# First stage of a hybrid decoder layer: how h is made, where conditioning is computed, and how its loads are queued

## The chip, the cores and the metric

One core of one Trainium2 chip runs the whole layer. The metric is device time in microseconds of one execution, the median of several runs. TensorE multiplies, VectorE (DVE in the rows), ScalarE (ACT) and GpSimd (POOL) work on rows of up to 128 partitions, and SyncE (SP) issues nearly all transfers.

## The reference

The layer takes x (1024 tokens by 1024 channels) and a conditioning vector c of 1024, all in float32:

```
shift, scale, gate = split(silu(c) @ ada_w + ada_b, 3)
h = rms_norm(x, norm_g) * (1 + scale) + shift
sq, sk, sv, sz, dq, dk, dv, dz, db, da, lq, lk, lv, lz, lr, mg = split(h @ w_in)
out = x + gate * ((g_sb * (y_sb @ proj_sb) + g_gdn * (y_gdn @ proj_gdn) + g_gla * (y_gla @ proj_gla)) @ w_out)
```

`rms_norm(x, g)` is x / sqrt(mean(x^2) + 1e-6) * g. The three mixers y are stick-breaking attention, a gated delta rule and gated linear attention, with four heads each; g_sb, g_gdn, g_gla are sigmoid gates of mg. The change touches only the first two lines, and the part of `h @ w_in` that goes with them.

## The kernel before

**Layout.** Channels lie on partitions and tokens along the row, so x, h and the result are eight tiles (k = 0 to 7) of 128 x 1024. Every large product is done in three passes with operands split in two exact parts: `split` (L149 to L156) lets ScalarE round a tile to `hi` (L151) and VectorE subtract for `lo` (L152).

**The first stage, in order.** SP issues the columns, c and the eight x tiles (L98 to L104). TensorE spreads c over the partitions, ScalarE makes silu of it (`c_row`, L146). The squares of x are made by ScalarE, for two tiles by GpSimd (L315), added in pairs by VectorE (L321), and summed over partitions by products with `ones` (L322): eight float32 products into two banks `ms`. `rstd` is exp(-0.5 ln(.)) on ScalarE (L324, L326).

Then one loop over k. `conditioning(j)` (L295 to L301) loads one 128 x 1024 tile of ada_w, transposed, into a `u6` buffer, of which there are two, and VectorE multiplies it with `c_row` and sums along the row into one column of `mod`; j = k is the shift and j = 8 + k the scale. The weights of the first delta-rule head for this k (four groups of 128 columns) come into one of three `raw` buffers (L339) and are split. The h tile is x times `rstd` on GpSimd (L363), then scaled and shifted on VectorE (L364) and split; tile 0 is done in halves without GpSimd (L353 to L358). TensorE then does 24 products of 512 columns per k: four groups, two halves, three passes, into eight banks. All h tiles stay in the 16 buffers of the tag `h` until the last projection.

**Behind the stage.** The eight banks are copied out, VectorE makes a causal convolution (L383, L386), and a small projection gives the gates of the delta rule (`small_evac`, L451 to L453 with GpSimd; Sigmoid, Exp and Ln on ScalarE; a scan, L473), whose transposes (`gates`, L122) and the tasks of the mixers follow, with the dense projections of the later heads as filler.

**What sets the order.** TensorE's instructions stand in the order in which the program writes them; for the mixers that order comes from estimated costs added up in `clock`, counted from the end of the first stage. The other engines and SP get an order from a planner that simulates the program and issues what it finds ready, in the program's order where several are; each engine then works through its list strictly in order. A buffer of a tag is given to the next tile of that tag once all users of an older one are done.

Of the kernel before, what the change touches and what calls it, by code (L numbers as in the profile page):

```python
# [12 lines left out]
F32 = mybir.dt.float32  # L13
# [6 lines left out]
P = 128  # L20
D = 1024
# [18 lines left out]
for _name, _n in (("norm_g", 8), ("ada_b", 24), ("sb_qnorm", 1), ("sb_knorm", 1), ("conv", 48),  # L40
                  ("gdn_onorm", 1), ("gla_b", 4), ("gla_onorm", 2), ("merge_b", 24),
                  ("a_log", 1), ("dt_bias", 1)):
    COLS[_name] = sum(v[1] for v in COLS.values()), _n
# [9 lines left out]
def kernel(ctx: ExitStack, tc: tile.TileContext, xT: bass.AP, c: bass.AP,  # L53
                             adaT: bass.AP, w_in: bass.AP, cols: bass.AP, consts: bass.AP,
# [44 lines left out]
    crow = big("u3")  # L99
# [39 lines left out]
    na = cp.tile([P, 1], F32, name="na")  # L139
    nc.scalar.activation(out=na[DA, :], in_=C("a_log")[DA, :], func=AF.Exp)  # L140
# [84 lines left out]
    # a dense group: (load, run); loads are issued one group ahead  # L225
# [77 lines left out]
    warm = cp.tile([P, 1], F32, name="warm")  # L303
    nc.scalar.activation(out=warm, in_=c_row[:, 0:1], func=AF.Square)
    nc.scalar.activation(out=warm, in_=warm, func=AF.Ln, bias=one_c)
    rstd = big("u5")
    ms = [bank(pl, "lv", HALF) for _ in range(2)]
    for k in range(KT):
        if k % 2 == 0:
            x2s = big("u4" if k < 4 else "u5")  # L310
        for hf in range(2):
            sl = slice(hf * HALF, (hf + 1) * HALF)
            if k % 2 == 0:
                if k in (2, 4):
                    nc.gpsimd.tensor_mul(out=x2s[:, sl], in0=xs[k][:, sl], in1=xs[k][:, sl])  # L315
                else:
                    nc.scalar.activation(out=x2s[:, sl], in_=xs[k][:, sl], func=AF.Square)
                continue
            x2 = mid(f"v{k // 2 % 2}")
            nc.scalar.activation(out=x2, in_=xs[k][:, sl], func=AF.Square)  # L320
            nc.vector.tensor_add(out=x2s[:, sl], in0=x2s[:, sl], in1=x2)  # L321
            mm(ms[hf], ones, x2s[:, sl], 858, start=(k == 1), stop=(k == KT - 1))  # L322
    for hf in range(2):
        nc.scalar.activation(out=rstd[:, hf * HALF:(hf + 1) * HALF], in_=ms[hf], func=AF.Ln,  # L324
                             scale=1.0 / D, bias=eps_c)
    nc.scalar.activation(out=rstd, in_=rstd, func=AF.Exp, scale=-0.5)  # L326
    amp = cp.tile([P, KT], F32, name="amp")

    # the first head's four column groups advance together as h arrives
# [3 lines left out]
               (pl, "lv"), (pl, "lv"))  # L333
    for k in range(KT):
        conditioning(k)
        conditioning(8 + k)
        raw = raw_tile()
        wsrc = w_in[k * P:(k + 1) * P, O_DQ:O_DQ + 4 * 512].rearrange("p (g n) -> p g n", g=4)
        nc.sync.dma_start(out=raw, in_=wsrc[:, :, 0:P])  # L339
        w = wp.tile([P, 2, 4, P], F32R, tag="w", name="w")  # L340
        if k == 0:
            nc.gpsimd.tensor_copy(out=w[:, 0], in_=raw)
            nc.vector.tensor_sub(out=w[:, 1], in0=raw, in1=w[:, 0].bitcast(F32))
        else:
            split(w[:, 0], w[:, 1], raw)
# [4 lines left out]
        if k == 0:  # L350
            for hf in range(2):
                sl = slice(hf * HALF, (hf + 1) * HALF)
                nc.vector.scalar_tensor_tensor(out=xs[k][:, sl], in0=xs[k][:, sl],  # L353
                                               scalar=amp[:, k:k + 1], in1=rstd[:, sl],
# [105 lines left out]
    for _ in run_cm(small_w, small_evac):  # L460
        pass
# [922 lines left out]
```

## Time and profile before

| | us |
|---|---|
| three runs | 1521.94, 1521.08, 1520.1 |
| median | 1521.08 |
| the profiled execution, first to last instruction | 1522.0 |
| TensorE busy in it | 1463.0 |
| VectorE, ScalarE, GpSimd busy | 861.8, 676.8, 175.8 |

The profiled execution has a span only, no time of its own beside it; the span lies 0.9 us above the median of the runs. Matmul rows overlap, so busy time of TensorE says that it has work, not how fast it works; the distance between the starts of two rows says that. A float32 product has two rows, one of the three-pass products one. "Idle before <-releaser" is the wait of an engine ahead of a row and what ended it.

### The profile page before, as it was taken

How to read it: one execution, taken by the hardware profiler on the slowest of the kernel's cores; microseconds unless marked ns; L12 is line 12 of the kernel's file. 1: busy time of each engine (PE TensorE's matmuls, PEld its weight loads, DVE VectorE, ACT ScalarE, POOL GpSimd, SP SyncE). 2: the span in 40 equal slices, each digit the busy share in tenths (PEclk: the TensorE clock that was granted, in tenths of full speed). 3: DMA queues.
4: the chain of work that ended last, by engine and by line, in shares of the span. 5: the costliest groups of instructions: out<-in, count | busy, mean ns of one | idle time of the engine just before them, and what ended most of it. 6: DMA issues, size and time to landing. Idle time of an engine off the chain costs nothing.

```text
span 1522.0 us, 26560 instructions
## 1 busy us (share of the span) xinstructions
PE 1463.0 (96%) x10564; PEld 1227.5 (81%) x10564; DVE 861.8 (57%) x1855; ACT 676.8 (44%) x1473; POOL 175.8 (12%) x306
## 2 busy tenths in 40 slices
PE   4898999999999999999999999999999999999998
PEld 1677787777778887978888999889988888888887
DVE  5978736557653666667666525563555226474621
ACT  4255845462652846556475524342444442322200
POOL 4231222223330000000000100000000000000000
PEclk8899999999999999999999999999999999999999
DMA  6644322131231211212121212111122334353342
GB/s 211 189 119 120 99 87 74 44 88 47 79 93 50 56 43 53 53 32 60 50 67 38 69 49 63 49 36 42 43 69 85 110 104 138 115 149 111 120 143 76
DMA packets 162470, 126.48 MB, mean 83 GB/s; under 512 B 23429, under 2 KB 139269, under 8 KB 162346
## 3 DMA queue, kind: packets, MB, share of 16 engines
q1 hardware_dynamic: 162202, 124.47, 27.9%
q8 instruction: 83, 1.36, 0.4%
q14 instruction: 41, 0.34, 0.1%
q10 hardware_dynamic: 144, 0.31, 0.1%
HBM read 99.80 MB, written 24.95 MB: 82 GB/s over the span
## 4 chain that ended last, share of the span: by engine, by line
PE 81%; DVE 9%; ACT 4%; POOL 2%; issue 2%; DMA 2%; SPq 0%; POOLq 0%; DVEq 0%; ACTq 0%
PE acc L95 66%; PE lv L95 6%; PE mx L95 6%; PE tr L122 3%; DVE u L299 1%; DVE w L152 1%; POOL c L284 1%; DVE u L386 1%; POOL u L453 1%; DVE w L570 1%; DVE w L572 1%; DVE u L1110 1%; DMA u<-in_adaT 1%; POOL w L596 0%; DMA w<-xd 0%
## 5 line engine op out<-in xcount | busy, mean ns | idle before, releaser
L95 PE MATMUL acc<-h_hi,w 128*128 128x512 f32 x1856 | 658.1, 409 | 12.4 <-ACT h_hi L151 5.7
L95 PEld LDWEIGHTS acc<-h_hi,w 128*128 128x128 f32 x1856 | 352.5, 190 | 84.5 <-ACT h_hi L151 6.1
L95 PE MATMUL acc<-h_lo,w 128*128 128x512 f32 x928 | 365.9, 394 | 8.1 <-DVE h_lo L358 7.7
L95 PEld LDWEIGHTS acc<-h_lo,w 128*128 128x128 f32 x928 | 176.9, 191 | 36.9 <-DVE h_lo L358 8.9
L95 PE MATMUL acc<-whi,h_hi 128*128 128x256 f32 x640 | 186.8, 292 | 0.0
L95 PE MATMUL acc<-whi,h_lo 128*128 128x256 f32 x640 | 180.7, 282 | 0.0
L95 PE MATMUL acc<-wlo,h_hi 128*128 128x256 f32 x640 | 180.7, 282 | 0.0
L95 PE MATMUL acc<-u,w 128*128 128x512 f32 x768 | 176.5, 391 | 0.0
L95 PEld LDWEIGHTS acc<-u,w 128*128 128x128 f32 x768 | 144.2, 188 | 31.6
L151 ACT CAST w<-raw 128x512 fp32r<-128x512 f32 x143 | 84.2, 619 | 121.8 <-PE acc L95 90.4
L152 DVE TENSOR_TENSOR w<-raw,w 128x512 fp32r<-128x512 f32 x143 | 98.5, 701 | 50.7 <-ACT w L151 49.9
L95 PEld LDWEIGHTS acc<-whi,h_hi 128*128 128x128 f32 x640 | 122.3, 191 | 1.4 <-issue 0.7
L95 PEld LDWEIGHTS acc<-wlo,h_hi 128*128 128x128 f32 x640 | 122.4, 191 | 0.1
L95 PEld LDWEIGHTS acc<-whi,h_lo 128*128 128x128 f32 x640 | 122.1, 191 | 0.0
L284 POOL TENSOR_TENSOR c<-c,mhalf 128x4 f32<-128x4 f32 (+1 forms) x56 | 54.7, 976 | 578.8 <-DVE c L282 577.4
L95 PE MATMUL acc<-m_hi,w 128*128 128x512 f32 x256 | 79.0, 389 | 0.0
L1110 DVE TENSOR_TENSOR_SCAN u<-u,zero_c 128x128 f32<-128x128 f32 (+7 forms) x32 | 43.4, 1356 | 36.1 <-ACT u L1108 36.1
L155 DVE SCALAR_TENSOR_TENSOR w<-raw,col,w 128x128 fp32r<-128x128 f32 x96 | 29.5, 349 | 55.3 <-ACT w L154 55.3
L95 PEld LDWEIGHTS mx<-r,u 128*128 128x128 f32 x288 | 44.1, 190 | 18.0 <-DVE r L751 4.9
L95 PEld LDWEIGHTS acc<-m_hi,w 128*128 128x128 f32 x256 | 48.0, 188 | 10.0
L95 PE MATMUL mx<-r,u 128*128 128x128 f32 x288 | 48.5, 281 | 6.3 <-POOL u L720 2.7
L95 PE MATMUL lv<-u,u 128*32 128x32 f32 (+5 forms) x528 | 49.2, 252 | 4.1 <-DVE u L653 4.1
(254 smaller groups left out, 2177.6 us busy)
## 6 DMA issues: line engine op xcount, KB each, us to landing
raw<-in_w_in SPq DMA_DIRECT2D x160, 256.0 KB, 3.0
u<-in_adaT SPq DMA_DIRECT2D x24, 512.0 KB, 3.5
g_dram<-v SPq DMA_DIRECT2D x36, 256.0 KB, 2.1
v<-g_dram SPq DMA_DIRECT2D x36, 256.0 KB, 2.6
u<-in_xT SPq DMA_DIRECT2D x16, 512.0 KB, 5.6
u<-y_dram SPq DMA_DIRECT2D x16, 512.0 KB, 3.8
v<-gam_d SPq DMA_DIRECT2D x16, 256.0 KB, 3.5
y_dram<-v SPq DMA_DIRECT2D x16, 256.0 KB, 2.0
```

Of the source, the lines that this page charges most:

```text
L95: return nc.tensor.matmul(out, lhsT=lhsT, rhs=rhs, **kw)
L122: nc.tensor.transpose(out=out, in_=in_, identity=ident[:k, :k])
L151: nc.scalar.copy(out=hi, in_=raw)
L152: nc.vector.tensor_sub(out=lo, in0=raw, in1=hi.bitcast(F32))
L155: nc.vector.scalar_tensor_tensor(out=lo, in0=raw, scalar=scale, in1=hi.bitcast(F32), op0=ALU.mult, op1=ALU.subtract)
L284: nc.gpsimd.tensor_tensor(out=out, in0=out, in1=mhalf[:, 0:n], op=ALU.pow)
L299: nc.vector.tensor_tensor_reduce(out=junk, in0=aw, in1=c_row, scale=1.0, scalar=0.0, op0=ALU.mult, op1=ALU.add, accum_out=mod[:, j:j + 1])
L386: nc.vector.scalar_tensor_tensor(out=t, in0=r[:, tap:tap + T], scalar=C("conv", j + tap), in1=t, op0=ALU.mult, op1=ALU.add)
L453: nc.gpsimd.tensor_scalar(out=gt[0][DA, sl], in0=raw[DA, :], scalar1=C("dt_bias")[DA, :], scalar2=None, op0=ALU.add)
L570: nc.vector.tensor_tensor(out=t3, in0=L3[:, w:16, j:w].broadcast_to([32, n, w]), in1=Xl3[:, j:w, 0:w].broadcast_to([32, n, w]), op=ALU.mult)
L572: nc.vector.tensor_sub(out=Xl3[:, w:16, 0:w], in0=Xl3[:, w:16, 0:w], in1=t3)
L1110: nc.vector.tensor_tensor_scan(om[:, 0:n][:, ::-1], om[:, 0:n][:, ::-1], zero_c.broadcast_to([P, n]), 1.0, ALU.mult, ALU.add)
```

## The change

- c is loaded as eight columns too (`c_col`), with silu on ScalarE; `crow` moves to a `u8` buffer. `na` (Exp) is computed later, ahead of the gates' Sigmoid.
- The squares: tile 0 on GpSimd, tiles 1 and 3 on VectorE, the others on ScalarE. Tiles 0, 1 and 2 go to TensorE alone, 3 to 5 as one sum, 6 and 7 as one sum in halves: ten products. `rstd` is Sqrt on ScalarE and `reciprocal` on VectorE, by halves; a one-column Sqrt (`root`) stands after the first squares.
- The conditioning tiles are loaded into buffers of the tag `h`, two per k, the first three pairs with their raw weights ahead of the loop. For k = 0 and 1 the tile comes in another layout (`adaP`) and TensorE multiplies it with `c_col`: eight products of one moving column per tile, into the one bank of the tag `tr`, ahead of the first h products. For k = 2 to 7 VectorE reduces as before, in place, with one addition for shift and scale.
- h is made for every k as it was for tile 0: VectorE multiplies x by amplitude and `rstd` in one instruction, ScalarE adds the shift and rounds, VectorE makes the low part from x, shift and `hi`. GpSimd has no part in it, nor in the split of tile 0's weights.

```diff
@@ columns: c also comes as eight columns of 128
-                  ("a_log", 1), ("dt_bias", 1)):
+                  ("a_log", 1), ("dt_bias", 1), ("c", 8)):
...
-    crow = big("u3")
+    crow = big("u8")
...
-    na = cp.tile([P, 1], F32, name="na")
-    nc.scalar.activation(out=na[DA, :], in_=C("a_log")[DA, :], func=AF.Exp)
+    c_col = cp.tile([P, KT], F32, name="c_col")
+    nc.scalar.activation(out=c_col, in_=C("c", 0, KT), func=AF.Silu)
...
-    warm = cp.tile([P, 1], F32, name="warm")
-    nc.scalar.activation(out=warm, in_=c_row[:, 0:1], func=AF.Square)
-    nc.scalar.activation(out=warm, in_=warm, func=AF.Ln, bias=one_c)
+    ms = [bank(pl, "lv", HALF) for _ in range(2)]
+    halves = [slice(hf * HALF, (hf + 1) * HALF) for hf in range(2)]
+    root = cp.tile([P, 1], F32, name="root")
+    def square(k, out, eng):
+        for sl in halves if k == KT - 1 else (slice(0, T),):
+            if eng is nc.scalar:
+                eng.activation(out=out[:, sl], in_=xs[k][:, sl], func=AF.Square)
+            else:
+                eng.tensor_mul(out=out[:, sl], in0=xs[k][:, sl], in1=xs[k][:, sl])
+        return out
+    def add_up(x2, start=False, stop=False):
+        for hf, sl in enumerate(halves):
+            mm(ms[hf], ones, x2[:, sl], 858, start=start, stop=stop)
+    for k, eng in ((0, nc.gpsimd), (1, nc.vector), (2, nc.scalar)):
+        add_up(square(k, big(("u4", "u4", "u5")[k]), eng), start=(k == 0))
+    nc.scalar.activation(out=root, in_=one_c, func=AF.Sqrt)
+    part, more = square(3, big("u6"), nc.vector), [big("u6"), big("u5")]
+    for k in (4, 5):
+        nc.vector.tensor_add(out=part, in0=part, in1=square(k, more[k - 4], nc.scalar))
+    add_up(part)
+    last = [square(k, big("u3"), nc.scalar) for k in (6, 7)]
     rstd = big("u5")
-    ms = [bank(pl, "lv", HALF) for _ in range(2)]
-    for k in range(KT):
-        if k % 2 == 0:
-            x2s = big("u4" if k < 4 else "u5")
-        for hf in range(2):
-            sl = slice(hf * HALF, (hf + 1) * HALF)
-            if k % 2 == 0:
-                if k in (2, 4):
-                    nc.gpsimd.tensor_mul(out=x2s[:, sl], in0=xs[k][:, sl], in1=xs[k][:, sl])
-                else:
-                    nc.scalar.activation(out=x2s[:, sl], in_=xs[k][:, sl], func=AF.Square)
-                continue
-            x2 = mid(f"v{k // 2 % 2}")
-            nc.scalar.activation(out=x2, in_=xs[k][:, sl], func=AF.Square)
-            nc.vector.tensor_add(out=x2s[:, sl], in0=x2s[:, sl], in1=x2)
-            mm(ms[hf], ones, x2s[:, sl], 858, start=(k == 1), stop=(k == KT - 1))
-    for hf in range(2):
-        nc.scalar.activation(out=rstd[:, hf * HALF:(hf + 1) * HALF], in_=ms[hf], func=AF.Ln,
-                             scale=1.0 / D, bias=eps_c)
-    nc.scalar.activation(out=rstd, in_=rstd, func=AF.Exp, scale=-0.5)
+    for hf, sl in enumerate(halves):
+        nc.vector.tensor_add(out=last[0][:, sl], in0=last[0][:, sl], in1=last[1][:, sl])
+        mm(ms[hf], ones, last[0][:, sl], 858, start=False, stop=True)
+        nc.scalar.activation(out=rstd[:, sl], in_=ms[hf], func=AF.Sqrt, scale=1.0 / D, bias=eps_c)
+        nc.vector.reciprocal(out=rstd[:, sl], in_=rstd[:, sl])
+    na = cp.tile([P, 1], F32, name="na")
     amp = cp.tile([P, KT], F32, name="amp")
 
-    # the first head's four column groups advance together as h arrives
+    PRE = 2
+    first_mod = bank(pt, "tr", HALF)
+    def both(ap, k):
+        return ap[:, k:k + 9:8]
+    def conditioning2(k):
+        tiles = [hp.tile([P, T], F32, tag="h", name="ada") for _ in range(2)]
+        if k < PRE:
+            for i, t in enumerate(tiles):
+                nc.sync.dma_start(out=t, in_=adaP[2 * k + i])
+            return lambda: by_product(k, tiles)
+        for i, t in enumerate(tiles):
+            j = 8 * i + k
+            nc.sync.dma_start(out=t, in_=adaT[j * P:(j + 1) * P, :])
+        return lambda: by_rows(k, tiles)
+    def by_product(k, tiles):
+        for i, t in enumerate(tiles):
+            at = 2 * k + i
+            for kk in range(KT):
+                mm(first_mod[:, at:at + 1], t[:, kk * P:(kk + 1) * P], c_col[:, kk:kk + 1], 120,
+                   start=(kk == 0), stop=(kk == KT - 1))
+        nc.vector.tensor_add(out=both(mod, k), in0=first_mod[:, 2 * k:2 * k + 2],
+                             in1=both(C("ada_b", 0, 24), k))
+    def by_rows(k, tiles):
+        for i, t in enumerate(tiles):
+            j = 8 * i + k
+            nc.vector.tensor_tensor_reduce(out=t, in0=t, in1=c_row, scale=1.0, scalar=0.0,
+                                           op0=ALU.mult, op1=ALU.add, accum_out=mod[:, j:j + 1])
+        nc.vector.tensor_add(out=both(mod, k), in0=both(mod, k), in1=both(C("ada_b", 0, 24), k))
     first = (O_DQ, O_DK, O_DV, O_DZ)
     f_ps = [[None, None] for _ in first]
     f_banks = ((pa, "acc"), (pa, "acc"), (pm, "mx"), (pm, "mx"), (pt, "tr"), (pl, "lv"),
                (pl, "lv"), (pl, "lv"))
+    raws, conds = [], []
     for k in range(KT):
-        conditioning(k)
-        conditioning(8 + k)
+        conds.append(conditioning2(k))
         raw = raw_tile()
         wsrc = w_in[k * P:(k + 1) * P, O_DQ:O_DQ + 4 * 512].rearrange("p (g n) -> p g n", g=4)
         nc.sync.dma_start(out=raw, in_=wsrc[:, :, 0:P])
+        raws.append(raw)
+        if k == 2:
+            break
+    for k in range(PRE):
+        conds[k]()
+    for k in range(KT):
+        if k >= 3:
+            conds.append(conditioning2(k))
+            raw = raw_tile()
+            wsrc = w_in[k * P:(k + 1) * P, O_DQ:O_DQ + 4 * 512].rearrange("p (g n) -> p g n", g=4)
+            nc.sync.dma_start(out=raw, in_=wsrc[:, :, 0:P])
+            raws.append(raw)
+        if k >= PRE:
+            conds[k]()
         w = wp.tile([P, 2, 4, P], F32R, tag="w", name="w")
-        if k == 0:
-            nc.gpsimd.tensor_copy(out=w[:, 0], in_=raw)
-            nc.vector.tensor_sub(out=w[:, 1], in0=raw, in1=w[:, 0].bitcast(F32))
-        else:
-            split(w[:, 0], w[:, 1], raw)
+        split(w[:, 0], w[:, 1], raws[k])
         nc.vector.scalar_tensor_tensor(out=amp[:, k:k + 1], in0=mod[:, 8 + k:9 + k], scalar=1.0,
                                        in1=C("norm_g", k), op0=ALU.add, op1=ALU.mult)
         hi = hp.tile([P, T], F32R, tag="h", name="h_hi")
         lo = hp.tile([P, T], F32R, tag="h", name="h_lo")
-        if k == 0:
-            for hf in range(2):
-                sl = slice(hf * HALF, (hf + 1) * HALF)
-                nc.vector.scalar_tensor_tensor(out=xs[k][:, sl], in0=xs[k][:, sl],
-                                               scalar=amp[:, k:k + 1], in1=rstd[:, sl],
-                                               op0=ALU.mult, op1=ALU.mult)
-                nc.scalar.activation(out=hi[:, sl], in_=xs[k][:, sl], func=AF.Identity,
-                                     bias=mod[:, k:k + 1])
-                nc.vector.scalar_tensor_tensor(out=lo[:, sl], in0=xs[k][:, sl],
-                                               scalar=mod[:, k:k + 1],
-                                               in1=hi[:, sl].bitcast(F32),
-                                               op0=ALU.add, op1=ALU.subtract)
-        else:
-            nc.gpsimd.tensor_mul(out=xs[k], in0=xs[k], in1=rstd)
-            nc.vector.tensor_scalar(out=xs[k], in0=xs[k], scalar1=amp[:, k:k + 1],
-                                    scalar2=mod[:, k:k + 1], op0=ALU.mult, op1=ALU.add)
-            split(hi, lo, xs[k])
+        for sl in halves if k == 0 else (slice(0, T),):
+            nc.vector.scalar_tensor_tensor(out=xs[k][:, sl], in0=xs[k][:, sl],
+                                           scalar=amp[:, k:k + 1], in1=rstd[:, sl],
+                                           op0=ALU.mult, op1=ALU.mult)
+            nc.scalar.activation(out=hi[:, sl], in_=xs[k][:, sl], func=AF.Identity,
+                                 bias=mod[:, k:k + 1])
+            nc.vector.scalar_tensor_tensor(out=lo[:, sl], in0=xs[k][:, sl],
+                                           scalar=mod[:, k:k + 1],
+                                           in1=hi[:, sl].bitcast(F32),
+                                           op0=ALU.add, op1=ALU.subtract)
...
+    nc.scalar.activation(out=na[DA, :], in_=C("a_log")[DA, :], func=AF.Exp)
     nc.scalar.activation(out=rows[DB, :], in_=rows[DB, :], func=AF.Sigmoid)
...
+    ada = a["ada_w"][0].reshape(KT, P, 24, P).transpose(2, 1, 0, 3).reshape(24, P, D)
...
+             "adaP": ada[[0, 8, 1, 9]]
```

## Rows read from the trace of the kernel before

**Rows 1.** The profiled page: busy time by engine, and TensorE in 40 slices (tenths)
```profile
PE 1463.0 (96%) x10564; PEld 1227.5 (81%) x10564; DVE 861.8 (57%) x1855; ACT 676.8 (44%) x1473; POOL 175.8 (12%) x306
...
PE   4898999999999999999999999999999999999998
```

**Rows 2.** Stretches: us, busy (x count) of PE, PEld, DVE, ACT, POOL; clock, DMA share, GB/s
```profile
20.00:40.00 20.00, 7.42 (x16) 3.98 (x15) 17.01 (x12) 6.71 (x9) 14.97 (x7) 0.68 0.29 83
...
400.00:1522.00 1122.00, 1108.64 (x8132) 949.24 (x8130) 591.94 (x1216) 475.53 (x1044) 59.21 (x117) 1.00 0.25 75
```

**Rows 3.** The chain of waits, 0 to 135 us: start, us, what
```profile
31.83 5.51 DVE h_lo L358 x2
37.34 3.30 DVE u L299
```

**Rows 4.** VectorE in order of time: start, us, line, operation [idle before <-releaser]
```profile
18.73 1.21 DVE L299 CUSTOM_DVE_ANT_0 u<-u,u 128x1024 f32<-128x1024 f32 x1
...
59.98 0.81 DVE L364 TENSOR_SCALAR u<-u,amp,mod 128x1024 f32<-128x1024 f32 x1
60.71 1.22 DVE L299 CUSTOM_DVE_ANT_0 u<-u,u 128x1024 f32<-128x1024 f32 x1
61.91 1.23 DVE L152 TENSOR_TENSOR h_lo<-u,h_hi 128x1024 fp32r<-128x1024 f32 x1
```

**Rows 5.** GpSimd in order of time
```profile
10.06 2.04 POOL L315 TENSOR_TENSOR u<-u 128x512 f32<-128x512 f32 x2 [8.03 <-DMA u<-in_xT]
...
25.61 20.58 POOL L363 TENSOR_TENSOR u<-u,u 128x1024 f32<-128x1024 f32 x7 [5.03 <-ACT u L326]
```

**Rows 6.** TensorE's products and weight loads (PEld) in order of time
```profile
15.25 7.19 PE L95 MATMUL lv<-u,ones 128*128 128x512 f32 x14 [0.48 <-DVE u L321]
17.11 0.20 PEld L95 LDWEIGHTS lv<-u,ones 128*128 128x128 f32 x1 [0.52 <-issue]
...
21.41 0.19 PEld L95 LDWEIGHTS lv<-u,ones 128*128 128x128 f32 x1 [0.24 <-issue]
...
27.33 0.74 PE L95 MATMUL acc<-h_hi,w 128*128 128x512 f32 x1 [4.89 <-ACT h_hi L356]
...
49.59 0.80 PE L95 MATMUL acc<-h_hi,w 128*128 128x512 f32 x1 [5.69 <-ACT h_hi L151]
...
58.02 0.39 PE L95 MATMUL acc<-h_hi,w 128*128 128x512 f32 x1
...
90.66 0.39 PE L95 MATMUL acc<-h_hi,w 128*128 128x512 f32 x1
```

**Rows 7.** ScalarE in order of time
```profile
7.47 1.15 ACT L317 ACTIVATE u<-u 128x512 f32<-128x512 f32 x2 [3.56 <-DMA u<-in_xT]
...
22.47 0.69 ACT L324 ACTIVATE u<-lv,eps_c 128x512 f32<-128x512 f32 x1 [0.17 <-PE lv L95]
23.18 1.28 ACT L326 ACT_TABLE_LOAD   x1
24.47 1.06 ACT L326 ACTIVATE u<-u 128x1024 f32<-128x1024 f32 x1
```

**Rows 8.** TensorE, products of 128 moving columns, later
```profile
142.11 1.05 PE L95 MATMUL lv<-u 128*128 128x128 f32 x8
```

**Rows 9.** Stretches of 4 us, columns as in rows 2
```profile
8.00:12.00 4.00, 0.00 (x0) 0.00 (x0) 0.34 (x1) 3.95 (x8) 1.94 (x2) 1.00 1.02 417
...
36.00:40.00 4.00, 2.88 (x7) 2.12 (x7) 4.00 (x2) 0.00 (x0) 4.00 (x3) 0.50 0.00 0
```

**Rows 10.** VectorE's groups by line and shape: busy, mean ns, idle before
```profile
L386 DVE SCALAR_TENSOR_TENSOR u<-u,col,u 128x1024 f32<-128x1024 f32 x36 | 46.1, 1291 | 0.1
```

**Rows 11.** The gates' chain behind the stage, GpSimd and TensorE
```profile
100.84 8.96 POOL L453 TENSOR_SCALAR u<-v,col 4x512 f32<-4x512 f32 x1
...
132.40 1.09 PE L122 MATMUL tr<-cst,u 128*128 128x128 f32 x4 [4.68 <-DVE gam_c L490]
```

**Rows 12.** DMA issues, 0 to 60 us: count, KB each, median us to landing
```profile
u<-in_adaT SPq DMA_DIRECT2D x10, 512.0 KB, 3.5
```

More of the change, by code (lines that the diff above doesn't have):

```diff
@@ L53 @@
 def kernel(ctx: ExitStack, tc: tile.TileContext, xT: bass.AP, c: bass.AP,
-                             adaT: bass.AP, w_in: bass.AP, cols: bass.AP, consts: bass.AP,
+                             adaP: bass.AP, adaT: bass.AP, w_in: bass.AP, cols: bass.AP, consts: bass.AP,
                              gla_w2: bass.AP, proj_sb: bass.AP, proj_gdn: bass.AP,
@@ L1361, in _columns @@
              "gla_onorm": tiles(a["gla_onorm"][0]), "merge_b": tiles(a["merge_b"][0]),
-             "a_log": rows(a["gdn_a_log"][0]), "dt_bias": rows(a["gdn_dt_bias"][0])}
+             "a_log": rows(a["gdn_a_log"][0]), "dt_bias": rows(a["gdn_dt_bias"][0]), "c": tiles(a["c"][0])}
     return np.concatenate([parts[n] for n in COLS], axis=1)
@@ L1367 @@
     a = {n: np.asarray(v) for n, v in inputs.items()}
-    feeds = {"xT": a["x"][0].T, "c": a["c"], "adaT": a["ada_w"][0].T, "w_in": a["w_in"][0],
+    ada = a["ada_w"][0].reshape(KT, P, 24, P).transpose(2, 1, 0, 3).reshape(24, P, D)
+    feeds = {"xT": a["x"][0].T, "c": a["c"], "adaP": ada[[0, 8, 1, 9]], "adaT": a["ada_w"][0].T, "w_in": a["w_in"][0],
              "cols": _columns(a), "consts": _constants(), "gla_w2": a["gla_w2"][0],
```

## The prediction

> **What bounds the kernel now.** I read the page first, the stretches second, the chain of waits third, and last the single rows of each engine. The page has TensorE busy for 96% of the span, and its lowest digits stand in the first slices [rows 1]. By stretches [rows 2], TensorE is busy for 7.4 of 20 us between 20 and 40 us and for 1108.6 of the last 1122. So the kernel is bound by TensorE nearly everywhere, and the first 58 us are where it waits. A microsecond won there reaches the end if nothing behind it gives it back, for TensorE's instructions stand in a fixed order.
>
> The chain of waits in that gap [rows 3] is VectorE's: two L358 take 5.51 us, one L299 takes 3.30, before the h of the second tile. The reader is to see that these are slow copies of cheap instructions. L299 takes 1.22 at 60.71; L358 makes half a row in 2.76 us, while at 61.91 a whole row of h_lo takes 1.23 [rows 4]. GpSimd explains it: seven L363 products run from 25.61 to 46.19, 2.94 us each [rows 5], and VectorE's instructions are stretched for as long. TensorE starts the first tile at 27.33, the second at 49.59 and the third at 58.02; from there a tile follows every 5.44 us (32.64 for six, 58.02 to 90.66, where the eighth ends) [rows 6].
>
> **The sum, part by part.**
>
> *The sum of squares.* The x tiles land about 1.3 us apart: GpSimd's squares wait for the third tile until 10.06 [rows 5], and the first square starts at 7.47 [rows 7]. By that spacing the eighth lands at 7.47 + 7 x 1.295 = 16.5. Now there are eight products with `ones`, two rows each, and the last 14 rows end at 22.44 [rows 6]; ten weight loads take 4.30 us from 17.11 to 21.41, so a product takes 0.86. After the change there are ten, but six of them (k = 0, 1, 2) can run while x still arrives, two take the sum of tiles 3 to 5, and only two wait for tiles 6 and 7. GpSimd's one square is now a whole row, two of the 1.02 us halves in rows 5, and the first product waits for it until about 9.6; six products, the first two at half rate, 1.7 us, end near 16.5; the pair of the middle sum near 18.2. For the last pair the path is half a square 0.57 (1.15 for two [rows 7]), half an addition 0.7 (a whole-row two-tensor instruction is 1.23 [rows 4]), and the product, which queues behind the middle pair: 18.2 + 0.86 = 19.1 and 19.9 for the halves.
>
> *The root.* Ln, a table load and Exp take 22.47 to 25.53 now [rows 7]. Afterwards: Sqrt per half, 0.69 as Ln has now, and a reciprocal on VectorE. The trace has no reciprocal. Its bounds are half of L364's whole-row 0.81 us, so 0.4, and the slowest 512-wide row, L358's 2.76 [rows 3, 4]; I take 0.75, near the 0.7 of half an addition, the plainest row of that width. The table for Sqrt is asked for early by `root`; at worst its 1.28 us [rows 7] stand in ScalarE's gap between the last square (17.7) and 19.1. Inverse roots: 20.5 and 21.4.
> The Trainium skill (ScalarE: Activation LUTs, What ACT_TABLE_LOAD costs) puts a switch of tables at about 1283 ns and a further drain of about 1380 ns. Here Exp starts at 24.47, 0.01 us after the load that began at 23.18, so the trace shows the first part and no drain behind it. By the page the removed load would be worth 1.4 us more; I go by the row.
>
> *Conditioning of tiles 0 and 1 on TensorE.* It takes four L299 reductions (1.2 us each where undisturbed) from VectorE and adds 32 one-column products to TensorE, ahead of the first tile's. No such product is in the trace. The nearest are four products of 128 moving columns, two rows each, in 1.05 us [rows 8], 0.26 per product; that is the upper bound at full rate, twice it at half rate, and zero the lower. I take 0.12, about half the upper, because the stationary operand has the same width and the moving one is nearly gone: 2 us for a tile's 16. The first tile's loads have landed by 18.73, when L299 reads them [rows 4]. The second's come after 0.25 + 1.0 MB more; at the 417 GB/s of rows 9 and the slower rate of the 512-byte pieces behind it, near 22.1. So tile 0's products run 19.9 to 21.9 and tile 1's 22.1 to 24.1. Everything on TensorE behind them waits, first of all the first tile.
>
> *The first tile.* After 21.9: addition and amplitude 0.15 and 0.16, two hand-overs 0.2, half a row of x times rstd 0.7 and h_hi 0.7 (half of 1.23 and Ln's 0.69 [rows 4, 7]): 23.8. TensorE's own order gives 24.1. Loads, the split of the weights on ScalarE instead of GpSimd, and the order in VectorE's queue can each put some tenths between; I take 25.0 (24 to 29).
>
> *The tiles after it.* Two tiles cost 10.9 us plus a slow start. Between 36 and 40 us, after long idling, the granted clock is 0.50 (the 1.2 GHz level), and the second tile, begun at 49.59 after 5.7 us without work, took 8.43 instead of 5.44 [rows 6, 9], some of it waiting for h_lo. I add 2.5 once. The second tile ends at 25.0 + 10.9 + 2.5 = 38.4, where it ends at 58.0 now: 19.6 won.
>
> *Can the rest keep the 5.44 pace?* VectorE per tile k = 2 to 7, each a little under its row's length because neighbours overlap: two reductions 2.3, additions and amplitude 0.3, weights' low part 0.6, L364's 0.7 replaced by a two-tensor instruction of a whole row (L386's kind, 1.29 long [rows 10], 1.2 in a sequence), h_lo 1.15: 5.6, against 5.44. That loses 1 us over six tiles, and tiles 0 and 1, without reductions, take about 3.3 each and put it some 4 ahead, which covers it. GpSimd is then out of the way; without that cover, the loss would be the 1 us. Loads: 1.25 MB per tile at 417 GB/s is 3.2 us, under 5.44. The price of queueing ahead is that raw weights from k = 3 on stand behind them in SP's queue: the last conditioning load would land near 38, and VectorE wants the fourth tile's weights near 37, about 8 before TensorE does; this costs VectorE 1 to 2 us of its head start and TensorE nothing.
>
> *Behind the stage.* TensorE meets the gates' chain next: GpSimd's L453 takes 8.96 us, and the transposes at 132.40 wait 4.68 [rows 11]. These hang on the end of the first stage and move with it. Moved `na` adds one Exp (0.2) and perhaps a table load 1.28 to ScalarE around it, and other instructions find a new order. I book 1.5 lost; from 0 (it lies in ScalarE's idle time) to 4.7 (as much again as the wait now).
>
> Sum: 58.0 - 38.4 - 1.5 = 18.1 won. The profiled span is 1522.0 us, 0.9 above the median 1521.1 and the highest listed run is 1521.9; no time around the span is shown, so I subtract from the median: **1503.0**. Its own range, 24 to 27 for the first tile and 0 to 4 behind: 1500 to 1508.
>
> **Rivals.**
>
> *The reciprocal is slow.* If half a row takes 2.8 us, like L358 now, instead of 0.75, two stand in VectorE's queue ahead of the first tile: 19.8 + 5.6 = 25.4, then 0.3 + 0.7 + 0.7, and the first tile starts at 27.3 or a little later, 2.5 to 3 later than above: 1506. For: nothing in the trace shows a division to be as cheap as a product. Against: the simple VectorE rows of this width take 0.7.
> The Trainium skill (VectorE: DVE Perf Modes, First, the fixed hardware budget) speaks for it: reciprocal is an iterative division with a repeat count of 8. An estimate from that page, eight cycles for each of 512 elements at 0.96 GHz, is 4.3 us a half; no run here shows it yet, and the first tile would start near 30, 5 us late, 1508.
>
> *The gain is given back behind the stage.* ScalarE's and VectorE's queues around the gates' chain come out worse by as much as L453's 8.96 us: half the gain goes, 1512. For: that chain waits on GpSimd, ScalarE and VectorE in turn and nothing there is spare. Against: it starts from TensorE's results, and its instructions are the same.
>
> *The loads do not run ahead (the other side).* If a conditioning load waits until the tile before it has given up its h buffer, each of six tiles is a loop: landing 3.5 [rows 12], two reductions 2.4, 0.3 for addition and amplitude, x times rstd 1.29, h_hi 1.1 (two half rows on ScalarE), h_lo 1.2: 9.8. From tile 1's h at 30.8 that ends at 89.6, plus 5.44 for TensorE: 95.1 against 90.66, so 1526, slower. It decides from 9.1 us per tile. For: 32 tiles of that tag pass through 16 buffers. Against: sixteen buffers hold all sixteen conditioning tiles, and two come free for each tile's pair.
>
> *It changes nothing*: the stage is bound by loads anyway. Against: the 4 MB of x have landed at 16.5, and rows 9 have no traffic at all between 36 and 40.
>
> **How the numbers follow.** Forecast 0.60, slow reciprocal 0.20, given back 0.11, loads not ahead 0.05, nothing 0.04. About 0.2% (3 us) is what a measurement of this kernel can tell from no change. The first three are faster and all but a few hundredths of "given back" stay so: 0.90 faster; 0.04 the same; 0.06 slower. The range takes in the start at 24 with a fast clock, 4 us below the forecast with a little gained behind the stage (1498), and reaches up to the given-back case (1512).
>
> **What would show it.** No L363-like products on GpSimd and no VectorE instruction of a whole row above 1.3 us after 20 us; the last `ones` product ends near 20; the first tile starts near 25 and the third near 38; 5.44 us per tile after that; the eighth ends near 72. A reciprocal far over 0.75, an h chain that waits for `in_adaT`, or a third tile later than 44 would prove steps wrong; so would a stage that ends at 72 with an end above 1508.

## The result and the profile after

The changed kernel is slower: 1534.4 us (median of 4 runs, 1534.0 to 1535.5) against 1520.6 for the kernel before on the same chip, ratio 1.0089 with an interval of 1.0074 to 1.0103. Forecast were 1503.0. The profiled execution took 1534.0 us, of which 1532.2 are the span.

The page hides the loss: TensorE is busy for 97% of the span, more than before [rows 1]. By stretches of 20 us (columns as in [rows 2]) TensorE of the kernel before was busy for 7.42 and 13.85 of 20 us in the first two of these and full from 60 to 100 us; after the change none of the four is full.

```profile
20.00:40.00 20.00, 16.86 (x72) 14.40 (x72) 16.77 (x22) 4.75 (x8) 0.20 (x2) 0.57 0.47 153
40.00:60.00 20.00, 16.75 (x66) 13.15 (x66) 14.75 (x26) 3.97 (x5) 0.00 (x0) 0.93 0.62 206
60.00:80.00 20.00, 12.96 (x42) 9.23 (x40) 14.64 (x28) 3.44 (x4) 0.00 (x0) 0.82 0.50 170
80.00:100.00 20.00, 14.66 (x47) 10.94 (x47) 13.24 (x25) 3.80 (x7) 2.33 (x2) 0.83 0.49 149
```

GpSimd's column (the fifth) is nearly empty: its 15 us of products are gone, as the change says. TensorE's rows, in order of time, answer to [rows 6]:

```profile
16.54 2.74 PE L95 MATMUL lv<-u,ones 128*128 128x512 f32 x6
19.12 3.63 PE L95 MATMUL tr<-c_col,ada 128*128 128x1 f32 x32
23.00 6.99 PE L95 MATMUL tr<-c_col,ada 128*128 128x1 f32 x32 [0.25 <-DVE mod L361]
32.27 0.79 PE L95 MATMUL acc<-h_hi,w 128*128 128x512 f32 x1 [2.28 <-ACT h_hi L406]
42.17 0.39 PE L95 MATMUL acc<-h_hi,w 128*128 128x512 f32 x1
47.61 0.39 PE L95 MATMUL acc<-h_hi,w 128*128 128x512 f32 x1
55.02 0.51 PE L95 MATMUL acc<-h_hi,w 128*128 128x512 f32 x1 [1.80 <-ACT h_hi L406]
68.29 0.80 PE L95 MATMUL acc<-h_hi,w 128*128 128x512 f32 x1 [4.25 <-ACT h_hi L406]
79.06 0.50 PE L95 MATMUL acc<-h_hi,w 128*128 128x512 f32 x1 [1.80 <-ACT h_hi L406]
89.54 0.50 PE L95 MATMUL acc<-h_hi,w 128*128 128x512 f32 x1 [1.41 <-ACT h_hi L406]
100.32 0.51 PE L95 MATMUL acc<-h_hi,w 128*128 128x512 f32 x1 [2.32 <-ACT h_hi L406]
108.48 0.39 PE L95 MATMUL acc<-h_hi,w 128*128 128x512 f32 x1
```

The `ones` products end at 19.28 (forecast 19.9). The h tiles k = 0 to 7 start at 32.27, 42.17, 47.61, 55.02, 68.29, 79.06, 89.54 and 100.32, and the eighth ends at 108.48. The third starts 10.4 us earlier than before (58.02), and then the pace of 5.44 is lost: 60.9 us for six tiles instead of 32.6 (a tile's time runs here from its first product to the first of the next). By the fifth tile the lead is gone: 68.29, before 58.02 + 2 x 5.44 = 68.90. The stage ends 17.8 us later than at 90.66.

Against the forecast the span is 28.3 us late (1532.2 for 1522.0 - 18.1 = 1503.9). The third tile was expected at 38.4 and starts at 47.61: 9.2 late, 7.3 of them with the first tile (25.0, measured 32.27). The six tiles after it cost 28.2 more than 32.6. Behind the stage 9.1 came back: from its end to the end of the span are 1423.7 us, before 1431.3, and I had booked 1.5 the other way. 9.2 + 28.2 - 9.1 = 28.3.

The head, in VectorE's row, then the granted clock (last column but two) in two stretches of it and in one of a later tile:

```profile
23.06 6.56 DVE L333 RECIPROCAL u<-u 128x512 f32<-128x512 f32 x2
```
```profile
20.00:24.00 4.00, 3.75 (x30) 3.66 (x29) 1.18 (x3) 1.13 (x3) 0.00 (x0) 0.87 1.05 376
24.00:28.00 4.00, 4.00 (x21) 4.00 (x20) 4.00 (x2) 0.62 (x1) 0.00 (x0) 0.50 0.63 210
...
68.00:72.00 4.00, 3.15 (x7) 2.16 (x8) 1.80 (x5) 0.24 (x1) 0.00 (x0) 0.50 0.63 229
```

A half of the reciprocal is 3.28 us. The one-column products of tile 0 take 3.63, those of tile 1 take 6.99 at half the clock, and both chains end near 30.

Of the 28.2 us lost over the six tiles, TensorE waits 11.6 ahead of tiles 3 to 7 (the five waits for h_hi above) and 5.2 behind their first products for h_lo. Most of the other 11.4 it is busy, but slower: behind such a wait the granted clock is 0.50 for a part of the tile, and over tiles 3 to 7 its mean is 0.67 to 0.81. A slow tile also ends later, and the couplings below hang on the end of a tile.

For the later tiles the chain of waits from 63 us on shows what a tile hangs on:

```profile
64.13 0.63 ACT w L151
64.78 0.69 DVE w L152
...
65.77 1.29 DVE u L403
67.06 1.14 DVE u L299
...
77.34 0.63 ACT w L151
77.99 0.70 DVE w L152
78.71 0.38 SPq L163
...
79.14 0.50 SPq L352
...
79.69 5.64 DMA ada<-in_adaT
85.36 1.23 DVE ada L367
```

Three couplings stand in it. **B**: the split of the weights of tile 6 (L151 on ScalarE, L152 on VectorE) needs a weight buffer that TensorE gives back with the end of tile 3, and it stands ahead of x times rstd (L403) of tile 4 on VectorE; the reductions of tile 4 were done at 62.6. **A**: the conditioning pair of tile 6 (L352 at 79.14) stands on SP behind raw weights (L163), whose buffer L152 frees; so it too hangs on the end of a tile, and then comes 5.64 us of landing and the whole h. **C**: reductions for the output gates (L299), work of the next stage, stand in VectorE's queue between L403 and h_lo, and their loads (L297) on SP ahead of pairs. In that place on VectorE they cost next to nothing (h_hi of tile 6 ends at 89.5, and h_lo starts at 89.56); what costs is their loads on SP. SP's rows show how late the first of the later pairs goes out (the forecast had the last one landing near 38): the raw weights of tiles 3 to 6 are all ahead of the pair of tile 3, though the program asks for that pair first. SP's own waits from 10 to 112 us (us in all, times, longest) show why: 31.9 us for raw weights' buffers, 3.6 for a pair's own buffer, and besides 13.1 in two rows of the gates' loads (L297):

```profile
43.80 0.39 SPq L392 DMA_DIRECT2D raw<-in_w_in  x1
44.23 0.97 SPq L352 DMA_DIRECT2D ada<-in_adaT  x2
```
```profile
SPq L392 <- DVE w L152: 19.7, 4, 10.3
SPq L163 <- DVE w L152: 12.2, 2, 6.9
...
SPq L352 <- DVE mod L367: 3.6, 1, 3.6
```

### The profile page after: what moved, and what is told of

It is laid out like the page before. It is cut to its first block, busy times and chain, and to the rows that moved or that the text cites. A ratio compares the mean times of both kernels' runs of the same rounds, so it can differ in the third digit from the quotient of the medians.

```text
span 1532.2 us, 26643 instructions
## 1 busy us (share of the span) xinstructions
PE 1480.8 (97%) x10632; PEld 1241.6 (81%) x10632; DVE 851.6 (56%) x1839; ACT 676.5 (44%) x1468; POOL 148.6 (10%) x295
## 4 chain that ended last, share of the span: by engine, by line
PE 80%; DVE 9%; ACT 3%; issue 3%; DMA 3%; POOL 2%; SPq 0%; POOLq 0%; DVEq 0%; ACTq 0%
PE acc L95 64%; PE lv L95 6%; PE mx L95 6%; PE tr L122 2%; DVE u L431 2%; PE tr L95 1%; DVE w L152 1%; DVE w L616 1%; DVE w L618 1%; POOL c L284 1%; DMA v<-gam_d 1%; DMA raw<-in_w_in 1%; DVE u L1156 0%; DMA xd<-w 0%; POOL w L642 0%
## 5 line engine op out<-in xcount | busy, mean ns | idle before, releaser
L151 ACT CAST w<-raw 128x512 fp32r<-128x512 f32 x144 | 84.9, 619 | 149.8 <-PE acc L95 90.3
L152 DVE TENSOR_TENSOR w<-raw,w 128x512 fp32r<-128x512 f32 x144 | 97.5, 688 | 56.5 <-ACT w L151 55.8
```

What stands on the lines that cost most here:

```text
L151: nc.scalar.copy(out=hi, in_=raw)
L152: nc.vector.tensor_sub(out=lo, in0=raw, in1=hi.bitcast(F32))
```

## The experiments

All but the last change the changed kernel; ratios are to the kernel before, run on the same chip. Gains against the changed kernel (ratio 1.0089, another chip) go by the ratios. An edit of place or order also lets the planner order the other instructions anew, so none of them moves one thing only.

**One coupling at a time.** First the pairs of all eight tiles are asked for ahead of the first h tile:

```diff
     for k in range(KT):
         conds.append(conditioning2(k))
+        if k >= 3:
+            continue
         raw = raw_tile()
...
-        if k == 2:
-            break
...
         if k >= 3:
-            conds.append(conditioning2(k))
             raw = raw_tile()
```


> All sixteen conditioning tiles are allocated and their loads issued before the first h tile, instead of three pairs ahead and the others each behind the h of the tile before; nothing else is edited. Theory A (loads): in the changed kernel a conditioning pair is issued only when the h of the tile before has its buffer, so each of tiles 3 to 7 is a loop of load, reductions, h, 11 us instead of 5.44. It expects the third to eighth tiles to follow each other at 5.5 to 6 us, the eighth to end near 80 us instead of 107, and a time near 1534 - 25 = 1509 us. Theory B (order): the splits of the weights stand two tiles ahead of h_hi in ScalarE's queue and wait there for TensorE; it expects a gain here only as far as that order changes with the edit. Theory C (VectorE's load): the eight reductions for the output gate (9.8 us) and the fused instructions make VectorE the bound; it expects at most 5 us of gain, near 1529.

Measured: 1523.7 us, ratio 1.0020 (1.0009 to 1.0031). Tiles 1 to 7 take exactly 5.44 each, but TensorE waits 12.9 us for the first h_lo. VectorE's order now has the reductions of tiles 2 to 4 ahead of it, and five h_lo instructions come in one piece:

```profile
PE acc L95 <- DVE h_lo L407: 12.9, 1, 12.9
```
```profile
44.78 4.99 DVE L407 SCALAR_TENSOR_TENSOR h_lo<-u,mod,h_hi 128x512 fp32r<-128x512 f32 x5
```

So the loads can run ahead, and the pace comes back with A out and B and C unedited: the stage ends at 91.8, some 10.5 us are won. The new order loses the rest at the head.

Next B alone, then B by another way (two tiles' weights share a buffer), then C alone:

```diff
+        if k:
+            with tc.issue_after(hi_ins.ins), tc.issue_after(lo_ins.ins):   # h of tile k-1
+                split(w[:, 0], w[:, 1], raws[k])
```
```diff
-        w = wp.tile([P, 2, 4, P], F32R, tag="w", name="w")
+        if k % 2 == 0:
+            w_pair = wp.tile([P, 2, KT, P], F32R, tag="w", name="w")
+        w = w_pair[:, :, 4 * (k % 2):4 * (k % 2) + 4, :]
```
```diff
-        nc.sync.dma_start(out=aw, in_=adaT[j * P:(j + 1) * P, :])
+        with tc.issue_after(stage_end[0]):     # the stage's last raw weights on SP
+            nc.sync.dma_start(out=aw, in_=adaT[j * P:(j + 1) * P, :])
...
+        with tc.issue_after(stage_end[1]):     # the stage's last h_lo on VectorE
+            nc.vector.tensor_tensor_reduce(out=junk, in0=aw, in1=c_row, ...
```


> The split of each tile's weights is queued behind the h of the tile before, on ScalarE and VectorE, by edges of issue order only; the loads are as in the changed kernel. Theory B (order) expects h_hi to stop waiting behind a split, tiles 3 to 7 at about 6 us each, and a time near 1512 us. Theory A (loads) expects tiles 3 to 7 still 9 to 11 us apart, with VectorE's reductions waiting for in_adaT, and 1528 to 1535 us. Theory C expects no more than 3 us of gain.

> Two tiles' split weights share one of the three weight buffers, so that a split finds room for six tiles instead of three and does not wait for TensorE; the loads are written as in the changed kernel. Theory B expects the 9 us waits of ScalarE's splits for TensorE to vanish, tiles 3 to 7 at about 6 us, and near 1512 us. Theory A expects the raw weights to come earlier, but the conditioning pairs still one behind the other: 8 to 11 us per tile and 1522 to 1533 us.

> The loads and reductions for the output gate (columns 16 to 23 of the conditioning) are queued behind the first stage on SP and VectorE; nothing else is edited. Theory C expects the stage to lose the 9.8 us of these reductions and what waits for their loads: 10 us or more gained, near 1523 us. Theories A and B expect 2 to 5 us, only where such a reduction stands in the chain of waits (4.15 us of load at 49.7 and 1.2 per tile): 1529 to 1532 us.

Measured: 1528.5 (1.0063, 1.0042 to 1.0083), 1531.2 (1.0071, 1.0054 to 1.0087) and 1532.2 (1.0079, 1.0058 to 1.0100); the stages end at 102.2, 106.6 and 103.0. Tiles 3 to 6 still take 10.2 to 10.5 us in the first of the three, 7.5 to 11.9 and 8.7 to 10.8 in the others. By the ratios B out wins 4.0 us, hardly clear of the noise, and C out 1.5, within it. With B out, the chain runs through C and A; with C out, through B and A. One turn of the loop with B out, 10.4 from pair to pair:

```profile
53.02 0.38 SPq L352
53.50 5.41 DMA ada<-in_adaT
58.93 1.23 DVE ada L367
...
60.60 1.28 DVE u L407
61.88 1.14 DVE u L299
63.43 0.42 SPq L352
```

A alone is taken off SP by giving the pairs to GpSimd's queue, buffers as they are:

```diff
-            nc.sync.dma_start(out=t, in_=adaT[j * P:(j + 1) * P, :])
+            nc.gpsimd.dma_start(out=t, in_=adaT[j * P:(j + 1) * P, :])
```


> The changed kernel with one edit: the conditioning pairs of tiles 2 to 7 are issued from GpSimd's DMA queue instead of SP's; buffers and the order in which they are handed out stay as they are. Theory A1 (a pair waits for nothing of its own; it stands on SP behind raw weights, which wait for VectorE to split an earlier tile, which waits for TensorE): four pairs go out as soon as GpSimd's small fills let them, near 40 us, the tiles from the fifth on take 5.5 to 7 us, the stage ends near 88 instead of 108 and the time is near 1518. Theory A2 (the pair waits for its h buffer, whatever the queue): tiles of 10 us again, 1532 to 1535.

Neither theory holds: 1539.1 (1.0115, 1.0099 to 1.0130), A2's pace but not its reason. The pairs of tiles 3 to 5 are out at 43.7, so no buffer held them back, and these tiles still start 12.3, 13.4 and 11.2 us behind the tile before, now by C and B: x times rstd of tile 3 waits for a gate reduction (L299) whose load takes 8.05 us, and that of tile 4 for a split of weights. Only later do pairs wait on GpSimd: that of tile 6 19.9 us for its buffer, the last one for a fill of a weight buffer (out at 94.5).

```profile
40.62 3.12 POOL L352 DMA_DIRECT2D ada<-in_adaT  x6
```
```profile
42.43 8.05 DMA u<-in_adaT
...
55.57 1.23 DVE u L299
...
69.68 0.69 DVE w L152
70.51 1.26 DVE u L403
```

**Two and three at once.** B and C out together, then all three, with the pairs left where the program asks for them:

> The changed kernel with both other couplings out at once: the split weights of a tile queue behind the h of the tile before on ScalarE and VectorE, and the output gates' loads and reductions stand behind the stage. The conditioning pairs stay where the program has them, on SP. Theory A (the pairs' late place is the cause by itself): 10 us per tile as in either edit alone, stage end 102, 1528. Theory D (three in-order couplings in the same loop, each by itself enough to hold a tile for 10 us, so that taking out one or the other alone shows little): with two out, the pair of a tile hangs on the h of two tiles before, some 11 us for two tiles, 5.6 to 6.5 per tile, stage end 80 to 86, 1510 to 1515.

> As that run, and the pairs of tiles 2 to 7 on GpSimd's DMA queue besides. Theory D: all three couplings are out; 5.5 to 6 us per tile except for the last pair, which stands behind a GpSimd fill that waits for a weight buffer (up to 10 us once); stage end 82 to 90, 1510 to 1517. Theory A (buffers handed out late, whatever queue and order): 10 us per tile, 1528.

Measured: 1518.3 (0.9980, 0.9968 to 0.9992) and 1523.0 (1.0023, 1.0008 to 1.0037). With B and C out, tiles 1 to 3 take 5.44, tile 4 6.1, tile 5 7.1 and the last two 9.2 and 9.3; the stage ends at 90.0. Pairs go out at 40.3, 44.8, 53.1, 59.6 and 67.5 from the same place in the program. So A where it stands didn't make the 10 us by itself: B and C out together win 16.6 us by the ratios, one at a time 4.0 and 1.5. Theory D's pace came out up to tile 4, its time was 3 us too hopeful, and its reason is not what holds the rest. From 47 us on the chain of waits runs through no pair but round VectorE, 7.11 us from one h_hi to the next:

```profile
56.10 1.16 ACT h_hi L412
...
58.49 0.68 DVE w L152
...
61.89 1.30 DVE u L409
63.21 1.16 ACT h_hi L412
```

VectorE works for 5.9 of these and waits 1.2 for h_hi of the tile that it has just multiplied. The h_hi of tile 7 then stands on ScalarE behind weight splits of the work behind the stage (78.46), which is B once more.

The second run misses D's range (1510 to 1517, stage end 82 to 90): its stage ends at 94.65, and taking A off SP besides wins nothing. Tile 7 waits 7.8 us. Its pair is out only at 72.33, behind GpSimd's fill of a weight buffer, where 10 had been allowed, and its reductions (79.18) stand behind splits for the small projection, whose load takes 5.65 from 73.13 on.

**Loads ahead and an order by hand.** The first edit above, the split of tile k behind h of tile k-1, and VectorE's reductions behind an h_lo:

```diff
+            with tc.issue_after(made[k - 2][1]):      # h_lo of tile k-2
+                conds[k]()                             # reductions of tile k
```


> All sixteen conditioning tiles queued ahead of the first h tile, and two edges of order: the reductions of tile k stand behind h_lo of tile k-2 on VectorE, the split weights of tile k behind h of tile k-1 on ScalarE and VectorE. Theory A (in the changed kernel the loads are tied to the h buffers, and where they are not, VectorE's order keeps h_lo of the first tile back): the first tile starts at 32 as before, h_lo waits no more than 2 us, every tile takes 5.44, the stage ends at 75.5 (32 + 8 x 5.44) and the time is 1508 (15 to 16 us under the run with the loads ahead alone, whose stage ended at 91.8). Rival C (VectorE has too much to do with the output gates' reductions beside 5.6 us per tile): tiles of 7 us, the stage ends near 88, 1519.

Measured: 1509.3 (0.9919, 0.9900 to 0.9937). The stage:

```profile
33.58 0.79 PE L95 MATMUL acc<-h_hi,w 128*128 128x512 f32 x1 [2.33 <-ACT h_hi L412]
...
83.54 0.39 PE L95 MATMUL acc<-h_hi,w 128*128 128x512 f32 x1
```

Some 26 us are won by the ratios against the changed kernel, with the same instructions in other places and another order. Theory A's 1508 came out, its stage end (75.5) did not, so the time was met in part by luck (1425.9 us behind the stage, where the forecast implies some 1431): the first tile started 1.6 later, and tiles 4 to 6 took 6.2 to 6.7 for the gate reductions among them (C), with VectorE busy all through a round of 6.64.

**The reciprocal.** Ln and Exp in its place, alone and with the order:

```diff
-        nc.scalar.activation(out=rstd[:, sl], in_=ms[hf], func=AF.Sqrt, scale=1.0 / D, bias=eps_c)
-        nc.vector.reciprocal(out=rstd[:, sl], in_=rstd[:, sl])
+        nc.scalar.activation(out=rstd[:, sl], in_=ms[hf], func=AF.Ln, scale=1.0 / D, bias=eps_c)
+    nc.scalar.activation(out=rstd, in_=rstd, func=AF.Exp, scale=-0.5)
```


> Only the reciprocal is undone: Ln and Exp on ScalarE as in the kernel before, instead of Sqrt on ScalarE and 2 x 3.28 us of reciprocal on VectorE. The inverse root would be there at 19.9 + 0.7 + 1.3 (table) + 1.1 = 23 instead of 29.6. Theory: the one-column products that end at 30.0 then hold the first tile, which starts at 30.5 instead of 32.3, and the loop of the loads takes over again: 10 us per tile from the fourth on, 1532 (2 us won). Rival (the reciprocal is the main cost and delays the h tiles that free the buffers): the loop begins 5 us earlier, and the time is 1528.

> The loads ahead, both edges of order, and Ln with Exp instead of the reciprocal. Theory: the first tile starts where the one-column products end, 30.5, then 5.44 per tile, the stage ends at 74, 1506. Rival (the slow reciprocal alone held the first tile): 27, and the end 1503.

Measured: 1537.4 (1.0093, 1.0070 to 1.0117) and 1507.5 (0.9910, 0.9893 to 0.9928). Alone it moves the first tile to 30.44 and wins nothing: the stage ends at 113.25. The engines' order came out otherwise: the last pair goes out at 90.26 instead of 84.21, on SP behind two gate loads whose issues stretch from 79.48 to 90.21. With the order fixed the first tile starts at 29.44 and the stage ends at 81.18, 2.4 earlier (74 was forecast); the intervals overlap. The one-column products hold the first tile at 29 to 30 then, as the first theory says.

**Conditioning on TensorE.** No tile conditioned there (`PRE = 0`), with order and Ln; then the gates' work behind the stage and the small split for gla_w later too, with none and with two tiles there:

> As the run with loads ahead, edges of order and Ln with Exp, but all tiles conditioned by VectorE's reductions, none on TensorE. If the one-column products cost TensorE more than they spare VectorE (3.6 and 7.0 us against four reductions of 1.2): the first tile starts near 25.5, VectorE needs 5.6 us per tile without a head start, the stage ends near 71, 1503. If VectorE is the bound without them: tiles of 6.5 to 7 us, the stage ends near 79, 1511, slower than with two tiles on TensorE.

> As the run with loads ahead, edges of order, Ln with Exp and no tile conditioned on TensorE, and besides the output gates' loads and reductions behind the stage and the small split for gla_w behind the sixth tile. If what still holds TensorE in the stage is the wait for ScalarE behind the gla_w split (5.3 us) and the gates' reductions on VectorE (some 3 us): the stage ends near 73 instead of 81.0, 1500. If the moved reductions cost as much behind the stage: 1506, no change against the run without this.

> The same with two tiles conditioned on TensorE (loads ahead, edges of order, Ln with Exp, gates' loads and reductions behind the stage, gla_w split later). Tiles five to seven took 6.4 to 6.7 us in the run without the last two edits; at 5.44 the stage ends near 77.5 instead of 81.2, 1504. If TensorE's one-column products cost more than they spare, this is 3 to 4 us slower than the run with none.

Measured: 1507.9 (0.9911, 0.9896 to 0.9925), 1501.7 (0.9868, 0.9853 to 0.9883) and 1506.5 (0.9902, 0.9887 to 0.9917). The first of them starts at 24.89 and gives the lead back: tile 2 starts at 42.14, tile 3 only at 51.96, and the stage ends at 81.0, where the two forecasts were 71 and 79. The second has neither wait and ends near its forecast (73, 1500):

```profile
24.20 0.79 PE L95 MATMUL acc<-h_hi,w 128*128 128x512 f32 x1 [5.26 <-ACT h_hi L414]
...
74.35 0.39 PE L95 MATMUL acc<-h_hi,w 128*128 128x512 f32 x1
```

With two tiles on TensorE everything else alike, the first starts at 31.35 and the stage ends at 79.68. So this part of the change costs 4.8 us here (1506.5 less 1501.7, runs of one chip); with the gates' work still in the stage it made no difference (1507.5 and 1507.9). The kernel without it is the fastest of all, 1.3% under the kernel before.

**One part alone on the kernel before.** Only h is changed: tiles 1 to 7 are made as the first was.

```diff
-            nc.gpsimd.tensor_mul(out=xs[k], in0=xs[k], in1=rstd)
-            nc.vector.tensor_scalar(out=xs[k], in0=xs[k], scalar1=amp[:, k:k + 1],
-                                    scalar2=mod[:, k:k + 1], op0=ALU.mult, op1=ALU.add)
-            split(hi, lo, xs[k])
+        for sl in (slice(0, HALF), slice(HALF, T)) if k == 0 else (slice(0, T),):
...  # x*amp*rstd on VectorE, h_hi on ScalarE with bias, h_lo fused on VectorE, as for k == 0
```


> The kernel before with one part of the change alone: h of tiles 1 to 7 made by one fused VectorE instruction, h_hi on ScalarE and a fused h_lo, as for the first tile; no GpSimd product of x and rstd. Loads, squares, root and conditioning stay as before. If GpSimd's products stretched VectorE (rows of 2.76 and 3.30 us): no VectorE row of a whole row above 1.3 us from 27 us on, the second tile starts near 36 instead of 49.6, 5.6 to 6 us per tile after it, the stage ends near 78 instead of 90.7, 1509. Rival (the second tile waits for loads or for the order, not for the stretched rows): the second tile near 46, 1518.

Measured: 1509.0 (0.9917, 0.9901 to 0.9934), as forecast. The longest VectorE row of a whole row is 1.29 us, the second tile starts at 35.45 and the stage ends at 78.83:

```profile
35.45 0.50 PE L95 MATMUL acc<-h_hi,w 128*128 128x512 f32 x1 [1.80 <-ACT h_hi L354]
...
78.83 0.39 PE L95 MATMUL acc<-h_hi,w 128*128 128x512 f32 x1
```

Here the first tile starts at 24.58, with the old squares, Ln and Exp, and with all conditioning on VectorE.

## Why the prediction was wrong

The reading of the kernel before was right: GpSimd's products stretched VectorE, and taking them away is worth 13 us by itself (last experiment), most of the 18 that I forecast for the whole change.

The step that failed is "Can the rest keep the 5.44 pace?": six tiles took 60.9 us for 32.6, and 28.2 of the 28.3 us that the forecast missed are there. It added up VectorE's work (5.6 per tile, right: the last run with two tiles on TensorE has rounds of 11.1 for two tiles) and SP's bytes, and took the order of the queues for given. Four things in it were wrong. The program queues three pairs ahead, not eight: from k = 3 on each pair is asked for in the round of its own tile, and on SP it goes out even later, behind raw weights. I argued from sixteen buffers and not from the line where the load stands. An instruction in an in-order queue costs what it waits for, not what it takes: a split of 0.69 us ahead of L403 puts the end of an earlier tile between a tile's reductions and its h. The sum left out the output gates' reductions, 1.2 us each, which the planner put among the others. And the 2.5 for a slow start of TensorE was booked once; five more tiles started behind a wait, and slower products cost most of 11.4.

The rival on the other side, loads that do not run ahead, came closest: a loop of 9.8, measured 10.1 per tile over six; 1526, measured 1534. Its headline is borne out: with all pairs asked for ahead seven tiles keep 5.44. Its mechanism is not what the runs show: the pairs of tiles 3 to 5 had their buffers and went out early from another queue, and it helped nothing. As the queues stood, A, B and C made the 10 us together; with B and C out and A untouched tiles 1 to 5 fall to 5.4 to 7.1. What each costs by itself stays open, since each edit brought a new order with it. I had given that side 0.05 for a mechanism I could see, and nothing for what the planner of the order does with new instructions.

Terms by their size:

- *The sum of squares*: right (19.28 for 19.9, the roots at 19.15 and 20.01). The rebuilt squares win little: the run with the old ones has its first tile at 24.58, the best run with the new ones at 24.20.
- *The first tile*: 32.27 for 25.0, from the next two terms. The 9.1 that came back behind the stage hide it in the total, by luck.
- *The root*: 3.28 per half for 0.75, over my upper bound of 2.76; the rival "the reciprocal is slow" was true. It hid behind the one-column products, and undoing it alone won nothing. The Trainium skill (VectorE: DVE Perf Modes, First, the fixed hardware budget) spoke for the rival, and the estimate from its page, 4.3, is above the 3.28 that the trace shows.
- *Conditioning on TensorE*: 0.23 per product at full clock (3.63 for 16) and 0.44 at half, for 0.12. The upper bounds, 0.26 and twice that, held. I halved the bound for the missing columns, but here the weight load sets the price. The 32 products end at 30.0, where I had 24.1.
- *Behind the stage*: 7.6 us came back where I booked 1.5 lost. GpSimd's row of the gates is 4.15 for 8.96 [rows 11], and TensorE's wait of 4.68 is gone; the granted clock is 1.00 from 120 to 140 us, where it was 0.83. In the run with the loads ahead alone the row takes 8.35 and the wait 4.38, and nothing comes back (1431.1). Why the row is shorter in some runs isn't shown. I had said that this chain moves with the end of the stage. It does not quite: from the end of the stage to the end of the span there are 1423 to 1431 us in these kernels.

## What to carry to other kernels

Busy time per tile is a bound from below only; read for each queue what stands ahead of the instruction that you count on, and what that waits for. Free buffers don't make a load run ahead: look where the program asks for it and what its queue holds ahead of it. When several in-order waits close the same loop, taking out one can show almost nothing where two show much (here 4.0 and 1.5 us, together 16.6), so test them together before calling one harmless, and time each part of a change alone.

## What was not expected of the hardware

A one-column float32 product costs its weight load here. 31 loads take 3.54 us beside products that take 3.63:

```profile
19.12 3.54 PEld L95 LDWEIGHTS tr<-c_col,ada 128*128 128x128 f32 x31 [0.24 <-issue]
23.00 6.90 PEld L95 LDWEIGHTS tr<-c_col,ada 128*128 128x128 f32 x32 [0.34 <-DVE mod L361]
```

And the granted clock fell to 0.50 (the 1.2 GHz level) while TensorE did nothing but these products: they began at full speed, its mean is 0.87 from 20 to 24 us, and 0.50 from 24 to 28, where TensorE was busy without a gap. In the kernel before, it had been at 0.50 after idling [rows 9].

A reciprocal of 128 x 512 float32 on VectorE takes 3.28 us, 4.8 times a half row of Ln on ScalarE (0.69 [rows 7]).
